# FF2 by seven block products in five chunks, with partial sums through DRAM

## The chip, the cores and the metric

The kernel runs on one core of a Trainium2 chip. The metric is the device time of one launch in microseconds, as a median of 3 runs. The kernel computes in fp32: TensorE multiplies numbers of a shorter format (fp32r), so each fp32 operand is split into a high and a low part, and each product takes three matmuls: high × high, high × low, low × high.

## The reference

One layer of a hybrid decoder on 512 tokens, width 2048. The change touches the channel sub-layer at its end:

```
h = rms_norm(x, g_pre_mlp) * (1 + sc2) + sh2
f = square(relu(h @ w_ff1)) @ w_ff2        # w_ff1: 2048 x 8192, w_ff2: 8192 x 2048
x = x + gt2 * rms_norm(f, g_post_mlp)
```

Below, FF1 is `h @ w_ff1`, `u` is its squared ReLU, FF2 is `u @ w_ff2`. Everything before (the attention and recurrence branches, their output projection) is the same in both kernels.

## The kernel before

**FF1** already uses a scheme of seven block products (after Strassen and Winograd): a 2×2 block matrix product takes 8 block products, or 7 if sums and differences of the blocks are formed first and the 7 results are added up afterwards. The two token halves (256 tokens each) and the two halves of the 2048 inputs make one operand; the weights of a *pair* of 128-wide column blocks make the other. There are 32 pairs. Products 1 and 2 need no token-side sums; for pairs 0 to 11 they are made early (kind "a", and a part before it), and the five others later (kind "b"). Pairs 12 to 31 make all seven at once (kind "c").

A *step* is one pair and a quarter of the inputs: `raw_load(s + 3)` asks for its weights three steps ahead, `forms(s + 2)` (L1273 to L1297) makes the weights' forms two steps ahead, and `group(s)` (L1328) issues the matmuls, 42 of 128x256 for kind "c", 30 for "b". The forms are: three sums on VectorE (L1290, L1293, L1294), the high parts on ScalarE (L1289, L1296), the low parts on VectorE (L1295, L1297). The high and low tiles `fh`, `fl` have two buffers each, so that ScalarE can write the forms of step s + 2 only when TensorE is done with step s. At a pair's end `pair_end` (L1347) adds up the products, applies ReLU and square, and writes `u` to DRAM (`ud`).

**FF2** is the plain product: for each of 2 halves of the output columns, 64 blocks of 128 rows of the weights, 2 blocks of 512 columns and 4 blocks of 128 tokens, three matmuls of 128x512 (`f2_mm`, L1439 to L1446), 3072 in all. The 8 PSUM banks hold the 8 sums of one half from its first block to its last. `u` is read back and split by `u_split` (L1436, L1437), the weights by L102 and L103. Beside FF2's first half VectorE also makes the dot products of `qdot` (L218) that give the modulation vectors. After the last matmul of each block of tokens `final` (L1464) scales the row and adds the residual, 16 instructions of 128x512.

The program is written in the order of the loops. A scheduler then chooses the order on each engine ahead of the run; on the chip each engine takes its own list in that order, and an instruction that waits holds up those behind it on the same engine. SyncE (SP) issues the loads, GpSimd (POOL) the writes of `u`.

Of the kernel before, what the change touches and what calls it, by code (L numbers as in the profile page):

```python
# [30 lines left out]
NA1, NA2, NMS, NFS, NTMP, NXI, NPC, NSB, TD, MRATE, NMD, NRT = 4, 8, 22, 18, 6, 4, 2, 11, 3, 0.8, 4, 6  # L31
NL = 2
# [98 lines left out]
def hybrid_block_kernel(ctx: ExitStack, tc: tile.TileContext, xT, c, vec, wada, wst, win, wv0, wv1,  # L131
# [1013 lines left out]
    def alpha_end(q, p, pool, tg, nb):  # L1145
        A.activation(P1[q], p[:, T1], AF.Copy)
        x = pool.tile([128, 256], F32, name="ax", tag=tg, bufs=nb)
        u = pool.tile([128, 256], F32, name="au", tag=tg, bufs=nb)
        V.tensor_add(x, p[:, T2], P1[q])
        relu2(q, 0, x, 1.0, u)  # L1150
        G.dma_start(ud[q][:, 0, T1], u)
# [161 lines left out]
    def open_banks(s):  # L1313
        if s >= len(GR) or GR[s] in asked:
# [251 lines left out]
```

## Time and profile before

| what | value |
|---|---|
| median of 3 runs | 2247.62 us (2246.13 to 2249.41) |
| profiled execution: its own time | 2245.18 us |
| profiled execution: span, first to last instruction | 2243.5 us |
| mean granted clock of TensorE | 0.986 of full speed |
| FF1's seven-product steps, last window | 1120 to 1518 us |
| FF2's matmuls | 1523.6 to 2234 us |
| end after the last matmul | 9.1 us |

The profile is of one execution. Times are microseconds unless marked ns. PE is TensorE's matmul side, PEld its weight loads, DVE is VectorE, ACT ScalarE. In a window's row, the first number after the stretch is its length, then each engine's busy time with its count of instructions; PEclk is the granted clock (1.00 is 2.4 GHz, 0.50 is 1.2 GHz). In a timeline's row the bracket gives the idle time ahead of the instruction and what ended it. Names like `fh` are buffers of the program, written output<-inputs; `ps_...` are PSUM banks.

### The profile page before, as it was taken

What the parts mean: (1) busy time and instruction counts of PE and PEld (TensorE: products, weight loads), DVE (VectorE), ACT (ScalarE), POOL (GpSimd) and SP (SyncE); (2) the same over time, 40 slices, a digit from 0 to 9 for tenths busy, and PEclk for the clock granted to TensorE, in tenths of its full rate; (3) what the DMA queues carried; (4) which work ended last, traced back from release to release, by engine and by line L of the source; (5) the groups of instructions that cost most, each with busy time, mean ns of one, the idle gap of its engine ahead of it and who ended that gap; (6) DMA issues with size and microseconds to landing.
All of it is one profiled execution on the core that took longest, in us unless ns stands there. A gap on an engine that the chain in (4) does not pass through costs nothing.

```text
span 2243.5 us, 33596 instructions
## 1 busy us (share of the span) xinstructions
PE 2161.5 (96%) x12317; PEld 1853.6 (83%) x12317; DVE 1590.0 (71%) x3260; ACT 1144.2 (51%) x2139; POOL 40.5 (2%) x81
## 2 busy tenths in 40 slices
PE   7997999999989988999999999998999999999998
PEld 3686878878867867999999999997888888888886
DVE  8977999878886768799988888876654334333333
ACT  4348889559983237655555555554323333333331
POOL 0000000000000000000000000000000000000000
PEclk9999999999999999999999999999999999999999
DMA  9755545741238885655544434437877444444433
GB/s 378 309 219 157 177 157 170 242 148 59 72 103 273 286 266 167 192 171 177 178 131 138 135 123 134 139 133 258 300 244 229 141 144 146 143 143 146 143 122 113
DMA packets 138982, 398.41 MB, mean 178 GB/s; under 512 B 18609, under 2 KB 19777, under 8 KB 134465
## 3 DMA queue, kind: packets, MB, share of 16 engines
q1 hardware_dynamic: 132546, 375.31, 51.5%
q0 software_dynamic: 6272, 20.98, 2.5%
q8 instruction: 96, 1.57, 0.3%
q14 instruction: 68, 0.56, 0.1%
HBM read 366.84 MB, written 29.38 MB: 177 GB/s over the span
## 4 chain that ended last, share of the span: by engine, by line
PE 66%; issue 24%; DVE 5%; ACT 3%; DMA 1%; POOL 0%; DVEq 0%; SPq 0%; POOLq 0%; ACTq 0%
PE ps_pj L1445 4%; PE ps_pj L1444 4%; PE ps_pj L1446 4%; PE ps_pj L1131 3%; PE ps_pj L1132 3%; PE ps_pj L1133 3%; PE ps_T L1446 3%; PE ps_T L1444 3%; PE ps_S L1445 3%; PE ps_S L1444 3%; PE ps_S L1446 3%; PE ps_T L1445 3%; PE ps_T L1131 2%; PE ps_T L1133 2%; PE ps_T L1132 2%
## 5 line engine op out<-in xcount | busy, mean ns | idle before, releaser
L102 ACT ACTIVATE sl<-wr 128x512 fp32r<-128x512 f32 (+2 forms) x388 | 228.9, 613 | 342.4 <-DMA wr<-wout 91.4
L103 DVE TENSOR_TENSOR sl<-wr,sl 128x512 fp32r<-128x512 f32 (+2 forms) x388 | 256.1, 671 | 188.2 <-ACT sl L102 173.8
L218 DVE SCALAR_TENSOR_TENSOR md<-md,ca 128x512 f32<-128x512 f32 x256 | 170.2, 686 | 59.2 <-DMA md<-wada 38.4
L1289 ACT ACTIVATE fh<-fr 128x768 fp32r<-128x768 f32 (+1 forms) x128 | 87.3, 682 | 227.7 <-PE ps_T L1132 89.6
L177 PE MATMUL ps_pj<-AH,sl 128*128 128x512 f32 x384 | 161.7, 421 | 0.0
L1297 DVE TENSOR_TENSOR fl<-fs,fh 128x1024 fp32r<-128x1024 f32 x128 | 156.4, 1222 | 3.7 <-ACT fh L1296 3.6
L103 DVE TENSOR_TENSOR AL<-wr,AH 128x512 fp32r<-128x512 f32 x120 | 81.7, 689 | 108.6 <-ACT AH L102 108.6
L102 ACT ACTIVATE AH<-wr 128x512 fp32r<-128x512 f32 x120 | 73.5, 626 | 164.2 <-PE ps_O L1446 68.4
L178 PE MATMUL ps_pj<-AL,sl 128*128 128x512 f32 x384 | 153.2, 399 | 0.0
L179 PE MATMUL ps_pj<-AH,sl 128*128 128x512 f32 x384 | 153.0, 398 | 0.0
L1437 DVE TENSOR_TENSOR AL<-ur,AH 128x1024 fp32r<-128x1024 f32 x64 | 78.4, 1224 | 103.9 <-ACT AH L1436 103.6
L1295 DVE TENSOR_TENSOR fl<-fr,fh 128x768 fp32r<-128x768 f32 (+1 forms) x128 | 96.5, 754 | 53.2 <-ACT fh L1289 53.1
L1296 ACT ACTIVATE fh<-fs 128x1024 fp32r<-128x1024 f32 x128 | 133.6, 1044 | 0.0
L1436 ACT ACTIVATE AH<-ur 128x1024 fp32r<-128x1024 f32 x64 | 67.7, 1058 | 83.7 <-PE ps_T L1445 79.6
L1132 PE MATMUL ps_pj<-tlt,fh 128*128 128x256 f32 x368 | 103.7, 282 | 0.0
L1131 PE MATMUL ps_pj<-AH,fh 128*128 128x256 f32 x352 | 99.1, 282 | 0.0
L1133 PE MATMUL ps_pj<-AH,fl 128*128 128x256 f32 x352 | 98.4, 280 | 0.0
L1290 DVE TENSOR_TENSOR fs<-fr 128x512 f32<-128x512 f32 x128 | 88.2, 689 | 5.2 <-DMA fr<-wff 2.1
L1444 PE MATMUL ps_pj<-sl,AH 128*128 128x512 f32 x204 | 81.4, 399 | 5.5 <-ACT sl L102 5.5
L179 PEld LDWEIGHTS ps_pj<-AH,sl 128*128 128x128 f32 x384 | 72.5, 189 | 16.3 <-DVE sl L103 0.6
L177 PEld LDWEIGHTS ps_pj<-AH,sl 128*128 128x128 f32 x384 | 72.8, 190 | 11.7 <-ACT tr L818 0.6
L1445 PE MATMUL ps_pj<-sl,AH 128*128 128x512 f32 x204 | 81.4, 399 | 0.5 <-DVE sl L103 0.5
(567 smaller groups left out, 6821.7 us busy)
## 6 DMA issues: line engine op xcount, KB each, us to landing
fr<-wff SPq DMA_DIRECT2D x144, 512.0 KB, 3.6
md<-wada SPq DMA_DIRECT2D x256, 256.0 KB, 4.9
wr<-wff SPq DMA_DIRECT2D x128, 512.0 KB, 3.8
ur<-ud SPq DMA_DIRECT2D x64, 512.0 KB, 3.4
wr<-win SPq DMA_DIRECT2D x48, 512.0 KB, 3.4
ada<-wada SPq DMA_DIRECT2D x22, 1024.0 KB, 10.3
wr<-wout SPq DMA_DIRECT2D x36, 512.0 KB, 4.7
ud<-ust POOLq DMA_DIRECT2D x20, 512.0 KB, 3.0
```

The source lines that it names most:

```text
L102: self.nc.scalar.activation(hi, raw, AF.Copy)
L103: self.nc.vector.tensor_sub(lo, raw, self.f(hi))
L177: T.matmul(o, wh, mh, start=start, stop=False)
L179: T.matmul(o, wl, mh, start=False, stop=stop)
L218: (V.scalar_tensor_tensor(w, w, 0.5, CA[0], op0=OP.mult, op1=OP.mult, accum_out=dq[s_][:, q_, k:k + 1]))
L1131: T.matmul(o, wh, b[0], start=start, stop=False, skip_group_check=True)
L1132: T.matmul(o, wh, b[1], start=False, stop=False, skip_group_check=True)
L1133: T.matmul(o, wl, b[0], start=False, stop=stop, skip_group_check=True)
L1297: V.tensor_sub(lo[:, 768:], Sm, f(hi[:, 768:]))
L1444: T.matmul(p, AH[:, k, hs], w[0], start=start, stop=False)
L1445: T.matmul(p, AH[:, k, hs], w[1], start=False, stop=False)
L1446: T.matmul(p, AL[:, k, hs], w[0], start=False, stop=stop)
```

## The change

FF2 also becomes seven block products. Its 32 pairs of rows of `u` are taken in five chunks (7, 7, 7, 7 and 4 pairs); in each chunk four groups of output columns n follow one another, so there are 20 groups, each of as many steps as the chunk has pairs: 128 steps (kind "f"). A step makes seven products of two token blocks with three matmuls of 128x256 each: 42, in all 5376. The seven sums of a group stand in 7 PSUM banks of the 8.

- **Between groups.** At a group's last step every sum is copied out of PSUM by ScalarE and written to DRAM by a DMA on POOL's queue (`bank_out`). The next group's banks are opened (`bank_open`): in the first chunk by a copy of 256 zeros, in the other four by a copy of the partial sum of the same n from the chunk before, which a DMA on ScalarE's queue has read back from DRAM (`p_in`, three buffers `pin`). The matmuls then add to what stands in the bank. In the last chunk `fin_step` adds the seven sums up instead of copying them out.
- **Weights.** `raw_load` and `forms` run over FF1's and FF2's steps in one list. For FF2 a step's high parts are one instruction of 128x1792 on ScalarE, and so are the low parts on VectorE.
- **Token side.** `pair_end` makes FF2's sums of `u` at the end of each of FF1's pairs (three new instructions on VectorE), and writes seven blocks, 917 KB a pair, to DRAM in place of four. `u_form` reads them back and splits them, one instruction of 128x1792 on ScalarE and one on VectorE for each pair: for pair 0 inside FF1, for six at FF2's start and in the first group, for the others in the last group of the chunk before.
- **End.** All 16 instructions of the final scaling stand after the last matmul.

```diff
--- before
+++ after
@@
-NA1, NA2, NMS, NFS, NTMP, NXI, NPC, NSB, TD, MRATE, NMD, NRT = 4, 8, 22, 18, 6, 4, 2, 11, 3, 0.8, 4, 6
-NL = 2
+NA1, NA2, NMS, NTMP, NXI, NPC, NSB, TD, MRATE, NMD, NRT = 4, 8, 22, 6, 4, 2, 11, 3, 0.8, 4, 6
+NPS, NFT, NXF = 5, 3, 6
...
-    ud = [dram.tile([128, 2, S], F32, name=f"ud{q}") for q in range(32)]
+    ud = [dram.tile([128, 1792], F32, name=f"ud{q}") for q in range(32)]
...
+    CH = [[*range(7 * i, 7 * i + 7)] for i in range(4)] + [[*range(28, 32)]]
+    for c_, pairs in enumerate(CH):
+        for n in range(4):
+            GR += [("f", (c_, n), p_) for p_ in pairs]
...
+        hi = wp.tile([128, 1792], F32R, name="fh", tag="fh", bufs=2)
+        lo = wp.tile([128, 1792], F32R, name="fl", tag="fl", bufs=2)
         FM[s] = hi, lo
+
+        def part(src, c0, n):
+            A.activation(hi[:, c0:c0 + n], src, AF.Copy)
+            V.tensor_sub(lo[:, c0:c0 + n], src, f(hi[:, c0:c0 + n]))
...
+        V.tensor_add(Sm[:, 1024:1536].rearrange("p (a b) -> p a b", a=2),
                      R[:, 256:768].rearrange("p (a b) -> p a b", a=2),
                      R[:, None, :256].to_broadcast([128, 2, 256]))
-        V.tensor_add(Sm[:, 512:768], Sm[:, :256], R[:, 512:768])
-        V.tensor_add(Sm[:, 768:], Sm[:, 512:768], R[:, 768:])
-        V.tensor_sub(lo[:, :n], R[:, 256:256 + n], f(hi[:, :n]))
-        A.activation(hi[:, 768:], Sm, AF.Copy)
-        V.tensor_sub(lo[:, 768:], Sm, f(hi[:, 768:]))
+        V.tensor_add(Sm[:, 1536:1792], Sm[:, 1024:1280], R[:, 512:768])
+        V.tensor_add(Sm[:, 1792:], Sm[:, 1536:1792], R[:, 768:1024])
+        if one and kind != "b":
+            part(R[:, 256:], 0, 1792)
+        else:
+            n = 256 if kind == "b" else 768
+            part(R[:, 256:256 + n], 0, n)
+            part(Sm[:, 1024:], 768, 1024)
...
+        V.tensor_sub(X[:, 4:6], X[:, 1:3], X[:, 0:1].to_broadcast([128, 2, 256]))
+        V.tensor_add(X[:, 6], X[:, 4], X[:, 2])
+        V.tensor_sub(X[:, 7], X[:, 6], X[:, 3])
...
+    FORD = (1, 2, 6, 7, 4, 5, 3)
...
+    def u_form(p_, sl):
+        u_load(p_)
+        u = UR.pop(p_)
+        hi, lo = US[p_] = SL[sl]
+        A.activation(hi, u, AF.Copy)
+        V.tensor_sub(lo, u, f(hi))
+        SLOT_OF[p_] = sl
...
+    def p_in(c_, n, i):
+        t_ = OPP["p"].tile([128, S], F32, name="pin", tag="pin", bufs=3)
+        nc.scalar.dma_start(t_, pd[n, i])
+        PI_[c_, n, i] = t_
+
+    def bank_open(c_, n, i):
+        b_ = PB2[c_, n, i] = bank()
+        if c_ == 0:
+            A.activation(b_[:, T2], zz, AF.Copy)
+        else:
+            A.activation(b_, PI_.pop((c_, n, i)), AF.Copy)
+
+    def bank_out(c_, n, i):
+        b_ = PB2.pop((c_, n, i))
+        t_ = OPP["p"].tile([128, S], F32, name="pst", tag="pst", bufs=NPS)
+        A.activation(t_, b_, AF.Copy)
+        G.dma_start(pd[n, i], t_)
...
+    def f2_mm(s, i):
+        _, (c_, n), p_ = GR[s]
+        l = FORD[i]
+        hi, lo = FM[s]
+        uh, ul = US[p_]
+        b_ = PB2[c_, n, i]
+        wc = slice(256 * SLOT[l], 256 * SLOT[l] + 256)
+        first, last = p_ == CH[c_][0], p_ == CH[c_][-1]
+        for t_ in range(2):
+            o = b_[:, 256 * t_:256 * t_ + 256]
+            c0 = 256 * UB[l] + 128 * t_
+            uh_, ul_ = uh[:, c0:c0 + 128], ul[:, c0:c0 + 128]
+            T.matmul(o, uh_, hi[:, wc], start=first and c_ == 0 and t_ == 0, stop=False, skip_group_check=True)
+            T.matmul(o, uh_, lo[:, wc], start=False, stop=False, skip_group_check=True)
+            T.matmul(o, ul_, hi[:, wc], start=False, stop=last, skip_group_check=True)
...
+            raw_load(s + 3)
+            forms(s + 2)
+            nq = (c_, n + 1) if n < 3 else (c_ + 1, 0)
+            if g == pairs[-2] and 0 < nq[0] < 5:
+                for i in range(3):
+                    p_in(*nq, i)
+            for i in range(7):
+                if g == pairs[0] and (c_, n, i) not in PB2:
+                    bank_open(c_, n, i)
+                f2_mm(s, i)
+                if g == pairs[-1]:
+                    if nq[0] < 5:
+                        bank_open(*nq, i)
+                        if nq[0] and i < 4:
+                            p_in(*nq, i + 3)
+                    if c_ < 4:
+                        bank_out(c_, n, i)
+                    else:
+                        fin_step(n, i)
...
+            if c_ == 0 and n == 0 and g < 5:
+                u_form(next(uord), frees.pop(0))
+                u_load(g + 3)
+            elif n == 2 and g == pairs[-1] and c_ < 4:
+                u_load(CH[c_ + 1][0])
+                u_load(CH[c_ + 1][1])
+            elif n == 3 and c_ < 4:
+                nx = CH[c_ + 1]
+                i = g - pairs[0] - (c_ == 3)
+                if 0 <= i < len(nx):
+                    u_form(nx[i], SLOT_OF[g])
+                    if i and i + 1 < len(nx):
+                        u_load(nx[i + 1])
+            if c_ < 3:
+                if qn < 64:
+                    qn += 1
+                    qdot(OPP["p"], 5, 1, ("pst", NPS))
...
-    def u_split(i):
-        if i < 64:
-            r_ = slice(2 * (i % 4), 2 * (i % 4) + 2)
-            u = UR.pop(i)
-            A.activation(AH[:, r_], u, AF.Copy)
-            V.tensor_sub(AL[:, r_], u, f(AH[:, r_]))
...
-    def f2_mm(h, m, fb, ch, free, start, stop):
-        w = ws.get(uf2[h, m], fb, free)
-        k = m % 8
-        hs = slice(128 * ch, 128 * ch + 128)
-        p = OB[fb, ch]
-        T.matmul(p, AH[:, k, hs], w[0], start=start, stop=False)
-        T.matmul(p, AH[:, k, hs], w[1], start=False, stop=False)
-        T.matmul(p, AL[:, k, hs], w[0], start=False, stop=stop)
...
+        rs = rs_of(FIN["p"], ssqf[:, ch])
+        for q in range(4):
+            mv = FIN["M"][:, ch, fbs(q)]
+            V.scalar_tensor_tensor(mv, mv, rs, XI.pop(0), op0=OP.mult, op1=OP.add)
+            nc.sync.dma_start(out[ch, :, fbs(q)], mv)
```

The first place is ScalarE in FF2. Before, its list holds the splits of `u` (`ur`) and of the weights (`wr`), nothing else:

```order
L1436 ACTIVATE AH_68<-ur_20279 128x1024
L102 ACTIVATE AH_68<-wr_20331 128x512 x2
L102 ACTIVATE AH_68<-wr_20365 128x512 x2
L1436 ACTIVATE AH_68<-ur_20347 128x1024
L102 ACTIVATE sl_20443<-wr_20395 128x512
L102 ACTIVATE sl_20459<-wr_20395 128x512
```

After, between two groups of the second chunk (line numbers are those of the changed kernel; `pst` takes a sum out, `pin` brings a seed in, `pd` is its place in DRAM, `fh_18664` is the high part of the weights two steps after the group's last):

```order
L1459 ACTIVATE pst_18681<-ps_S_18246 128x512
L1459 ACTIVATE pst_18694<-ps_T_18259 128x512
L1454 ACTIVATE ps_S_18690<-pin_18613 128x512
L1454 ACTIVATE ps_T_18703<-pin_18615 128x512
L1446 DMA pin_18692<-pd_9261 128x512
L1446 DMA pin_18705<-pd_9261 128x512
L1303 ACTIVATE fh_18664<-fs_18602 128x1792
L1459 ACTIVATE pst_18707<-ps_S_18272 128x512
L1459 ACTIVATE pst_18720<-ps_T_18285 128x512
L1454 ACTIVATE ps_S_18716<-pin_18679 128x512
L1454 ACTIVATE ps_T_18729<-pin_18692 128x512
L1446 DMA pin_18718<-pd_9261 128x512
```

Between the first two copies out and the others now stands the making of a weight form; two of the seven seeds' loads are issued ahead of it and one behind it, in ScalarE's list.

The second place is VectorE at the end of a pair of kind "b" in FF1. Before:

```order
L1362 TENSOR_TENSOR X_10988<-ps_O_10747,p1_5_9215 128x256
L1293 TENSOR_TENSOR fs_11033<-fs_11033,fr_10976 128x256
L1364 TENSOR_TENSOR X_10988<-ps_S_10748,X_10988 128x512
L1295 TENSOR_TENSOR fl_10979<-fr_10929,fh_10978 128x256
L1365 TENSOR_TENSOR X_10988<-ps_T_10749,X_10988 128x512
L1297 TENSOR_TENSOR fl_10979<-fs_10980,fh_10978 128x1024
L1366 TENSOR_TENSOR X_10988<-ps_S_10748,X_10988 128x256
```

After, at the same pair, from its last sum out of PSUM on (`uf` is the tile that `X` was, L1399 and L1400 are what L1365 and L1366 were):

```order
L1399 TENSOR_TENSOR uf_10824<-ps_T_10759,uf_10824 128x2x256
L1400 TENSOR_TENSOR uf_10824<-ps_S_10758,uf_10824 128x256
L1315 TENSOR_TENSOR fs_10984<-fs_10984 128x256
L1304 TENSOR_TENSOR fl_11042<-fs_10984,fh_11041 128x256
L1316 TENSOR_TENSOR fs_10984<-fs_10984 128x256
L1312 TENSOR_TENSOR fs_11039<-fs_11039 128x512
L1315 TENSOR_TENSOR fs_11039<-fs_11039 128x256
L1411 TENSOR_TENSOR uf_10824<-uf_10824 128x512
L1316 TENSOR_TENSOR fs_11039<-fs_11039 128x256
L1412 TENSOR_TENSOR uf_10824<-uf_10824 128x256
L1304 TENSOR_TENSOR fl_11042<-fs_10984,fh_11041 128x1024
L1413 TENSOR_TENSOR uf_10824<-uf_10824 128x256
```

L1411, L1412 and L1413 are new; the last two stand on either side of a low part of the weights (L1304) that TensorE's next steps read.

## Rows read from the trace of the kernel before

**Rows 1.** The top of the page: the span; busy time, share and instructions.

```profile
span 2243.5 us, 33596 instructions
...
PE 2161.5 (96%) x12317; PEld 1853.6 (83%) x12317; DVE 1590.0 (71%) x3260; ACT 1144.2 (51%) x2139; POOL 40.5 (2%) x81
```

**Rows 2.** Windows of FF1 and FF2, columns as in the first line.

```profile
core 0: us, PE busy (x) PEld busy (x) DVE busy (x) ACT busy (x) POOL busy (x), PEclk, DMA share, GB/s
950.00:1120.00 170.00, 169.92 (x1432) 169.92 (x1433) 163.04 (x288) 90.68 (x155) 12.32 (x23) 1.00 0.57 176
1120.00:1518.00 398.00, 398.00 (x3363) 397.93 (x3361) 330.75 (x473) 208.66 (x294) 11.18 (x21) 1.00 0.42 132
1518.00:1523.50 5.50, 0.14 (x2) 0.00 (x0) 2.38 (x5) 3.63 (x6) 0.53 (x1) 0.79 0.32 102
1523.50:1528.00 4.50, 3.86 (x8) 2.77 (x9) 4.32 (x6) 2.76 (x6) 0.00 (x0) 0.50 0.81 254
1528.00:2234.40 706.40, 706.22 (x3065) 574.51 (x3063) 301.57 (x479) 224.91 (x348) 0.00 (x0) 1.00 0.55 175
2234.40:2243.50 9.10, 0.00 (x0) 0.00 (x0) 3.65 (x7) 0.90 (x3) 0.00 (x0) 0.70 0.66 247
```

**Rows 3.** Windows, a stretch of FF2 with more transfers.

```profile
1555.00:1700.00 145.00, 145.00 (x631) 118.09 (x631) 86.32 (x184) 43.13 (x66) 0.00 (x0) 1.00 0.83 273
```

**Rows 4.** Timeline of PE at the start of FF2: start, us, instruction.

```profile
1523.59 0.80 PE L1444 MATMUL ps_pj<-sl,AH 128*128 128x512 f32 x1 [5.46 <-ACT sl L102]
...
1526.38 0.63 PE L1445 MATMUL ps_pj<-sl,AH 128*128 128x512 f32 x1
1526.81 0.63 PE L1446 MATMUL ps_pj<-sl,AL 128*128 128x512 f32 x1
```

**Rows 5.** Timeline of DVE, one step of FF1.

```profile
1492.49 0.43 DVE L1294 TENSOR_TENSOR fs<-fs,fr 128x256 f32<-128x256 f32 x1
```

**Rows 6.** Timeline of ACT, the same step and the next.

```profile
1493.19 0.85 ACT L1289 ACTIVATE fh<-fr 128x768 fp32r<-128x768 f32 x1 [3.18 <-PE ps_O L1132]
1493.94 1.04 ACT L1296 ACTIVATE fh<-fs 128x1024 fp32r<-128x1024 f32 x1
...
1498.16 0.85 ACT L1289 ACTIVATE fh<-fr 128x768 fp32r<-128x768 f32 x1 [2.91 <-PE ps_O L1132]
```

**Rows 7.** Groups of ACT by form: count | busy us, mean ns | idle before.

```profile
L1289 ACT ACTIVATE fh<-fr 128x768 fp32r<-128x768 f32 x80 | 67.3, 841 | 160.6 <-PE ps_O L1132 82.2 <-PE ps_T L1132 78.4
...
L1296 ACT ACTIVATE fh<-fs 128x1024 fp32r<-128x1024 f32 x128 | 133.6, 1044 | 0.0
...
L1324 ACT ACTIVATE ps_pj<-zz 128x256 f32<-128x256 f32 x31 | 11.6, 374 | 0.3
...
L847 ACT ACTIVATE y<-ps_pj 128x512 f32<-128x512 f32 x8 | 4.8, 594 | 0.0
```

**Rows 8.** Groups of DVE by form, the same columns.

```profile
L218 DVE SCALAR_TENSOR_TENSOR md<-md,ca 128x512 f32<-128x512 f32 x256 | 170.2, 686 | 59.2 <-DMA md<-wada 38.4 <-DMA ca<-cad 17.5 <-issue 2.5
L1297 DVE TENSOR_TENSOR fl<-fs,fh 128x1024 fp32r<-128x1024 f32 x128 | 156.4, 1222 | 3.7 <-ACT fh L1296 3.6
L1290 DVE TENSOR_TENSOR fs<-fr 128x512 f32<-128x512 f32 x128 | 88.2, 689 | 5.2 <-DMA fr<-wff 2.1
...
L1295 DVE TENSOR_TENSOR fl<-fr,fh 128x768 fp32r<-128x768 f32 x80 | 76.5, 956 | 53.0 <-ACT fh L1289 53.0
...
L1464 DVE SCALAR_TENSOR_TENSOR M<-M,rs,xin 128x512 f32<-128x512 f32 x16 | 11.0, 746 | 0.1
```

**Rows 9.** DMA issues: queue, count, KB each, median us to landing.

```profile
md<-wada SPq DMA_DIRECT2D x256, 256.0 KB, 4.9
...
ada<-wada SPq DMA_DIRECT2D x22, 1024.0 KB, 10.3
...
wr<-wff SPq DMA_DIRECT2D x16, 256.0 KB, 2.7
```

**Rows 10.** The 64 loads of md in FF2: time to landing.

```profile
DMA to landing us min/median/max: 3.8/5.6/7.2
```

More of the change, by code (lines that the diff above doesn't have):

```diff
@@ new lines, in hybrid_block_kernel, with u_load @@
+    SL = {i: (AHf[:, 1792 * i:1792 * i + 1792], ALf[:, 1792 * i:1792 * i + 1792]) for i in range(4)}
+    UR, US = {}, {}
+    ulist = [p_ for c_ in CH for p_ in c_]
+    def u_load(p_):
+        if p_ < 32 and p_ not in UR:
+            UR[p_] = uf_tile().rearrange("p a b -> p (a b)")[:, :1792]
+            nc.sync.dma_start(UR[p_], ud[p_])
+    def u_form(p_, sl):
[5 more added lines that the diff above has]
+        SLOT_OF[p_] = sl
@@ new lines, in hybrid_block_kernel, with tmp, v2, fin_step @@
+    FIN = {}
+    def tmp(name):
+        return FIN["p"].tile([128, S], F32, name=name, tag="tmp", bufs=NFT)
+    def v2(ap):
+        return ap.rearrange("p (a b) -> p a b", a=2)
+    def fin_step(n, i):
+        l = FORD[i]
+        b_ = PB2.pop((4, n, i))
+        M = FIN["M"]
+        d1, d2 = slice(256 * n, 256 * n + 256), slice(1024 + 256 * n, 1280 + 256 * n)
+        W_ = FIN["w"]
+        def done(j, half):
+            for t_ in range(2):
+                ch = 2 * j + t_
+                mv = M[:, ch, (d1, d2)[half]]
+                A.activation(tmp("sq")[:, :256], mv, AF.Square, accum_out=ssqf[:, ch, 2 * n + half:2 * n + half + 1])
+            mv = M[:, 2 * j:2 * j + 2, (d1, d2)[half]]
+            V.scalar_tensor_tensor(mv, mv, (1.0, -1.0)[half], gbc2[0][:, None, (d1, d2)[half]].to_broadcast([128, 2, 256]),
+                                   op0=OP.mult, op1=OP.mult)
+        if l == 1:
+            W_[1] = tmp("w1")
+            A.activation(W_[1], b_, AF.Copy)
+        elif l == 2:
+            V.tensor_add(M[:, 0:2, d1], v2(b_), v2(W_[1]))
+            done(0, 0)
+        elif l == 6:
+            V.tensor_sub(W_[1], W_[1], b_)
+        elif l == 7:
+            W_[3] = tmp("w3")
+            V.tensor_add(W_[3], b_, W_[1])
+        elif l == 4:
+            V.tensor_add(M[:, 0:2, d2], v2(b_), v2(W_[3]))
+            done(0, 1)
+        elif l == 5:
+            V.tensor_add(M[:, 2:4, d2], v2(b_), v2(W_[3]))
+            V.tensor_add(W_[1], b_, W_[1])
+            done(1, 1)
+        else:
+            V.tensor_add(M[:, 2:4, d1], v2(b_), v2(W_[1]))
+            done(1, 0)
@@ L1390, in hybrid_block_kernel @@
             hst.close()
-            FP2["p"] = gst.enter_context(tc.tile_pool(name="fp2", bufs=1, side="right", reuse_waits="tile"))
+            RP["p"] = pool(rst, "rp", side="right")
         open_banks(s + 2)
         forms(s + 2)
+        if RP and "u" not in RP and not any(v[1] is None for v in RAW.values()):
+            frs.close()
+            RP["u"] = pool(rst, "ufp", side="right")
         if kind == "a":
@@ L1491, in hybrid_block_kernel @@
-    u_split(63)
-    x1_load(0)
+            if kind == "b" and q == NA1 + NA2 - 1:
+                ast.close()
+                xst = ExitStack()
+                xp = pool(xst, "xp", side="right")
+                SL[4] = tuple(xp.tile([128, 1792], F32R, name=f"us4{x}") for x in "hl")
+            if q == 29:
+                u_form(0, 4)
+            if q == 30:
+                u_load(1)
     for ch in range(4):
```

225 lines of the change are left out of this document (112 added, 113 removed).

## The prediction

> **What bounds the kernel now.** I read the top of the page first: PE is busy 96% of a span of 2243.5 us, VectorE 71%, ScalarE 51% [rows 1]. So the span is the matmuls' time plus a few gaps, and the question for each stage is whether something else comes late there. The windows answer it [rows 2]. FF1's "c" steps (1120 to 1518) keep PE busy all of 398.00 us with 3363 matmuls of 128x256: 118.35 ns each. FF2 (1528 to 2234.4) keeps it busy 706.22 of 706.40 us with 3065 matmuls of 128x512: 230.5 ns each. PE's gaps around FF2 are 5.5 us ahead of it, some 4.5 us at granted clock 0.50 (1.2 GHz) right after, and 9.1 us behind it. The matmul rate decides both stages, and in both every form is ready in time.
>
> Who has room? In the "c" stretch ScalarE is busy 208.66 of 398 us (52%), VectorE 330.75 (83%); in the "b" stretch ahead of it (950 to 1120) VectorE has 163.04 of 170, 7 us free [rows 2]. In FF2 both have more than half free. Most of the arithmetic of the change is therefore paid for; what it changes is that FF2 gets seams.
>
> **FF2's matmuls.** Before: 3072 in 1523.5 to 2234.4, 710.9 us with the slow start. After: 5376 of 128x256, the shape and step (42 matmuls) of FF1's "c" pairs. 5376 × 118.35 ns = 636.2. Difference **−74.7**. A step takes 42 × 0.11835 = 4.97 us, which is also the distance of the two L1289 in [rows 6]; one product of a step takes 0.71.
>
> **FF2's start.** The 5.5 us ahead of FF2 are the first forms, made when FF1 has ended (PE waited 5.46 us for a split [rows 4]). Now they are made in FF1's last steps by the same list that feeds FF1: **−5** (0 to −5.5).
>
> **The seams, 16 with seeds.** Within a group a step is like a "c" step. At a group's end seven sums must leave their banks and seven seeds enter, on ScalarE, whose list is fixed. What a fixed list does is seen in one FF1 step: the sums were there at 1492.92 [rows 5], their split L1296 started at 1493.94, because L1289 ahead of it waited for PE to finish the step whose buffer it takes, to 1493.19 [rows 6]. The list of the changed kernel has at a seam: out 0, 1; open 1, 2; loads 4, 5; the form of step L + 2 (L is the group's last step); out 2, 3; open 3, 4; load 6; then out 4, 5, open 5, out 6, open 6. That form has the place of L1289: it waits until PE has ended step L, since `fh` has two buffers. So five copies out and four openings stand behind the moment E at which L ends, and PE goes on meanwhile into L + 1.
>
> Durations: the form of 128x1792 on ScalarE 1.044 + 3 × 0.203 = 1.65 (0.203 is the difference of the 1024 and 768 rows [rows 7]); a copy out 0.59 as the 128x512 row out of PSUM; a copy in 0.37 for 256 [rows 7], for 512 estimated 0.58. Then, after E: form to 1.7; out 2 to 2.3, out 3 to 2.9, open 3 to 3.45. L + 1 wants bank 3 at 3 × 0.71 = 2.13: 1.3 to 1.4 late. Open 4 to 4.05, in time for the shifted product. Out 4, 5, open 5 to 6.15, wanted at 4.9: 1.3 late. Load 6 is issued at about 4.4; loads of 256 KB landed in 2.7 us in one place [rows 9] and in 5.6 (at most 7.2) in FF2 [rows 10]: the seed is there at 7.1 to 10.0, bank 6 open at 7.7 to 10.6, wanted at 6.9: 0.8 to 3.7 late. Sum 3.5 to 6.4 a seam. I take 6.0, by the loads in FF2, since the stage is loaded at least as much now. 16 × 6.0 = **+96** (56 to 102; each engine in order, so nothing gives a gain). In the last chunk's three seams the final sums stand in place of the copies out; I count them alike.
>
> **Three seams with zeros** (first chunk): copies out as above, but no load; what is late is bank 3 and bank 5, with 0.37 in place of 0.58: some 2 each, **+6** (0 to 15).
>
> **Chunk turns.** 31 pairs of `u` get their forms within FF2, five or six in a row, one a step. VectorE per step: sums 0.69 + 0.43 + 0.43 [rows 5, 8], low part of 1792 = 1.222 + 3 × 0.266 = 2.02 (the rows for 1024 and 768 differ by 0.266 [rows 8]), in all 3.57; the low part of `u` adds 2.02, a `qdot` 0.69: 5.6 to 6.3 us where PE needs 4.97. That is 0.6 to 1.3 us lost a step once the two steps' lead is used up: 31 × 0.62 = 19, 31 × 1.3 = 40, less what the lead saves in five places. Transfers there: 7 × (0.52 + 0.92) MB of weights and `u` plus 3.7 MB of sums out and in = 13.8 MB in 35 us of matmuls. 273 GB/s went with a DMA share of 0.83 [rows 3], so all engines busy would be 329 GB/s: 42 us. The two overlap. **+18** (0 to 35).
>
> **The clock.** After 5.5 us with hardly a matmul the next window shows a granted clock of 0.50, and a matmul of 128x512 every 0.43 us (1526.38, 1526.81) where 0.23 is usual [rows 2, 4]: nine matmuls × 0.2 = 1.8 us lost. A seam's idle comes in three pieces of 1 to 4 us, so not each will drop the clock: 16 × 1.0 = **+16** (0 to 29).
>
> **FF1.** Each "b" pair gets three more VectorE instructions, 0.69 + 0.42 + 0.42 = 1.53 us (the 512 row, and the 256 form twice). 12 × 1.53 = 18.4, where 7 us are free: **+14** (11.4 to 18.4). VectorE has 17% free in the "c" stretch, but there the additions sit between low parts that PE waits for, 20 pair ends × 0.3 = **+6** (0 to 7). Both only cost: PE has no idle left to give back there.
>
> **The end.** 12 more of the final instructions behind the last matmul, 0.746 each [rows 8] = 9, and the last squares: **+10** on the 9.1 there are.
>
> **Sum** on the profiled execution: −74.7 − 5 + 96 + 6 + 18 + 16 + 14 + 6 + 10 = +86.3; span 2243.5 + 86.3 = 2329.8. That execution took 2245.18, 1.7 more than its span, and the median of the runs is 2247.62, 2.4 above it: **2334 us**.
>
> **Rivals.**
> *A: the seams are hidden.* FF2 is as bound by matmuls as FF1. For it: the same shapes ran 398 us without a gap at ScalarE 52% busy [rows 2]. Against it: a form behind a wait for PE stands in the middle of ScalarE's list at each seam. −74.7 − 5 + 14 + 10 = −55.7: 2243.5 − 55.7 + 4.1 = 2192. It decides if out 2 to 6 are done within a step, which needs the form behind them. This is the other side: faster.
> *B: the seams cost their cheap end* (loads land in 2.7, clock and turns hidden): −74.7 − 5 + 56 + 14 + 10 = +0.3, 2248.
> *C: transfers bound the seams.* Seeds land as the 1 MB loads did, 10.3 us [rows 9], since they queue behind weights and sums. Bank 6 opens at 4.4 + 10.3 + 0.6 = 15.3, 8.4 late; a seam is 11.1, 16 × 5.1 = 82 more: 2416. For it: DMA share 0.83 in a stretch of FF2 now [rows 3]; against it: 256 KB loads in that same stretch landed in 5.6 [rows 10].
> *D: the clock stays at 1.2 GHz for the step after each seam.* 19 × 4.97 = 94 in place of 16: 2412. For it: the drop at FF2's start came from a single gap; against it: it lasted some 4.5 us, under one step, and came after 5.5 us of idle in one piece [rows 2]. The Trainium skill, "TensorE: Matmul & The Clock Gate", section "A second HAM failure mode: psum-queue depth-cycling", tells of a kernel that cycles through PSUM banks and whose short idle times between groups of matmuls were enough to make the clock swing between its two levels; by that rule D happens at each seam, and no stretch of the trace before has such groups.
>
> **How the numbers follow.** Forecast 0.75, A 0.07, B 0.06, C 0.07, D 0.05. Ends of the forecast's own range: seams at 56 with the clock's 0 give 2278, turns at 35 with the clock's 29, seams at 102 and FF1's upper ends 2375. A is left out of the range and about half of C and D; B is taken in: 2247 to 2410. A measurement of this kernel tells 0.2% (4.5 us) from no change: faster 0.09 (A and a part of B), same 0.04 (B), slower 0.87.
>
> **What would show it.** In the profile after: about 118 ns a matmul within a group; PE idle at 19 places, each some 6 us in three pieces, released by ScalarE's openings and, for the last bank, by the load of the seed; the granted clock below 1.00 only there; no gap between FF1 and FF2; a longer stretch of VectorE-bound steps at "b" pairs and in each chunk's last group. If ScalarE's openings are done before PE wants their banks, I am wrong in the largest term, and A or B holds. If the seeds' DMAs release nearly all of the idle time, C is right; if PE has no long idle but the clock reads 0.50 within steps, D.

## The result, and the profile after

The changed kernel took 2375.91 us (median of 4 runs, 2370.18 to 2385.83), the kernel before 2247.75 (4 runs). The ratio is 1.0575, 95% interval 1.0533 to 1.0617: slower, and by 128 us where 86 were forecast.

The top of the page after, for [rows 1]:

```profile
span 2369.5 us, 38792 instructions
...
PE 2150.9 (91%) x14621; PEld 1952.7 (82%) x14621; DVE 1877.2 (79%) x3528; ACT 1315.9 (56%) x2199; POOL 94.1 (4%) x181
```

PE has 2304 more matmuls and is yet busy 10.6 us less, but 91% of the span in place of 96%. The stretches that answer [rows 2], in its columns (the b pairs, the c pairs, the passage from FF1 to FF2, FF2, the end):

```profile
973.00:1137.00 164.00, 152.67 (x1231) 147.45 (x1229) 147.44 (x276) 81.56 (x145) 5.32 (x10) 1.00 0.55 188
1180.00:1540.00 360.00, 359.59 (x3037) 359.39 (x3036) 310.91 (x416) 185.70 (x201) 9.57 (x18) 1.00 0.46 158
1544.00:1551.00 7.00, 7.00 (x61) 7.00 (x60) 6.86 (x9) 4.47 (x6) 0.00 (x0) 1.00 0.83 263
1551.00:2338.60 787.60, 680.02 (x5341) 663.12 (x5339) 554.77 (x705) 396.30 (x459) 60.57 (x113) 0.95 0.65 219
2339.00:2369.50 30.50, 0.00 (x0) 0.00 (x0) 15.47 (x30) 3.51 (x16) 0.00 (x0) 0.55 0.68 224
```

The c pairs are full as before. At the passage PE works without a gap. In FF2 PE is busy 680.0 of 787.6 us at a mean clock of 0.95. After the last matmul's end follow 30.8 us, where it was 9.3.

By stages of the profiled execution (126.0 us longer in span): up to the first b pair's end 5.5; b pairs 21.8 (from the first pair's end to the last's: 156.3 before, 178.2 after); c pairs 1.3; FF2 with its start 75.9 (716.1 from FF1's end to the last matmul's end, 792.0 after); the end 21.5. The first of these can't be put down to the change: the two programs have the same rows in the same order up to some 945 us, and in two kernels that are like the changed one so far (e10 and e2, below) it was 1.4 and 10.3.

FF2's 792.0 us are 636.2 for 5376 matmuls at full clock, 106.9 of idle PE (the 68 waits in the timeline added up), and a rest of 49. Of the rest, 11 belong to the waits too: the matmul ahead of a wait is shown for 0.28 us, where the next one would have started after 0.118. So waits cost 118 us. The other 38 are matmuls that follow one another more slowly than at full clock. The idle time, in the waits of PE (total, times, longest):

```profile
PE ps_T L1477 <- DVE fl L1304: 32.0, 9, 8.6
PE ps_pj L1477 <- DVE fl L1304: 20.0, 10, 4.9
PE ps_S L1477 <- DVE fl L1304: 13.2, 10, 3.4
PE ps_pj L1476 <- ACT ps_pj L1454: 11.8, 11, 2.9
PE ps_S L1476 <- ACT ps_S L1454: 6.0, 6, 2.1
```

L1477 are the matmuls that take the weights' low part, L1476 the first ones, which wait for an opened bank (L1454). The prediction's waits at openings are there, 21 us in all banks, but the waits for low parts come to 70. Some 12 more are waits for high parts.

A seeded seam as predicted, in the fourth chunk. ScalarE's timeline (L1303 form, L1459 out, L1454 open, L1446 the seed's load):

```profile
2158.17 1.70 ACT L1303 ACTIVATE fh<-fs 128x1792 fp32r<-128x1792 f32 x1 [1.31 <-PE ps_pj L1478]
2159.78 0.58 ACT L1459 ACTIVATE pst<-ps_T 128x512 f32<-128x512 f32 x1
2160.25 0.59 ACT L1459 ACTIVATE pst<-ps_S 128x512 f32<-128x512 f32 x1
2160.73 0.60 ACT L1454 ACTIVATE ps_T<-pin 128x512 f32<-128x512 f32 x1
2162.57 0.60 ACT L1454 ACTIVATE ps_S<-pin 128x512 f32<-128x512 f32 x1 [1.24 <-DMA pin<-pd]
2162.60 0.33 ACTq L1446 DMA_DIRECT2D pin<-pd  x1
...
2168.81 0.60 ACT L1454 ACTIVATE ps_pj<-pin 128x512 f32<-128x512 f32 x1 [3.62 <-DMA pin<-pd]
```

and PE's waits in the same place:

```profile
2161.39 0.39 PE L1476 MATMUL ps_T<-fh,us4h 128*128 128x256 f32 x1 [0.74 <-ACT ps_T L1454]
...
2163.23 0.39 PE L1476 MATMUL ps_S<-fh,us4h 128*128 128x256 f32 x1 [0.86 <-ACT ps_S L1454]
...
2169.46 0.39 PE L1476 MATMUL ps_pj<-fh,us4h 128*128 128x256 f32 x1 [2.90 <-ACT ps_pj L1454]
```

The form starts when PE is done with the group's last step; out 2, out 3, open 3 follow; then the openings wait for seeds; the last seed, asked for at 2162.60, is used at 2168.81. PE loses 0.74, 0.86 and 2.90, three pieces, 4.5 us; the prediction had 1.4, 1.3 and 0.8 to 3.7.

What it did not have is seen in the first chunk, between groups without seeds. SyncE's issues, VectorE's rows, and PE's:

```profile
1594.20 1.65 SPq L217 DMA_DIRECT2D md<-wada  x3
1595.94 0.83 SPq L1291 DMA_DIRECT2D fs<-wff  x1
1596.94 6.66 SPq L217 DMA_DIRECT2D md<-wada  x4
```

```profile
1599.38 0.69 DVE L218 SCALAR_TENSOR_TENSOR md<-md,ca 128x512 f32<-128x512 f32 x1 [3.06 <-DMA md<-wada]
...
1601.79 0.69 DVE L218 SCALAR_TENSOR_TENSOR md<-md,ca 128x512 f32<-128x512 f32 x1 [1.71 <-DMA md<-wada]
...
1602.99 0.69 DVE L218 SCALAR_TENSOR_TENSOR md<-md,ca 128x512 f32<-128x512 f32 x1 [0.50 <-DMA md<-wada]
...
1603.61 2.02 DVE L1304 TENSOR_TENSOR fl<-fs,fh 128x1792 fp32r<-128x1792 f32 x1
```

```profile
1605.69 0.58 PE L1477 MATMUL ps_T<-fl,AH 128*128 128x256 f32 x1 [4.94 <-DVE fl L1304]
```

The scheduler put seven `qdot` loads (L217) in a row at the seam. A load's tile belongs to the ring of the copies out (`pst`), so it waits for a copy's write to DRAM. The weights' load (L1291) stands between and behind them on SyncE, and on VectorE the low part (L1304) stands behind three dot products that wait for their data. PE idles 4.94 us. Over FF2 these two waits are, on SyncE and on VectorE:

```profile
SPq L217 <- DMA pd<-pst: 60.3, 34, 7.1
```

```profile
DVE fs L1312 <- DMA fs<-wff: 106.5, 54, 11.5
```

Not all of this waiting reaches PE. Traced back to VectorE's last idle time ahead of each late low part, 32 of the 70 us stand behind a dot product that waited for its data, 29 behind sums that waited for weights.

The clock: at such a wait the granted clock falls to 0.50 (1.2 GHz), and behind it the matmuls of 128x256 follow each other by 0.21 us, where 0.118 is usual. First the window around the wait of 4.94 us above, then PE's rows at another:

```profile
1604.80:1611.60 6.80, 5.91 (x27) 5.92 (x28) 6.80 (x13) 0.00 (x0) 0.00 (x0) 0.50 0.39 127
```

```profile
1962.84 0.58 PE L1477 MATMUL ps_T<-fl,AH 128*128 128x256 f32 x1 [5.39 <-DVE fl L1304]
...
1963.43 0.41 PE L1476 MATMUL ps_T<-fh,AH 128*128 128x256 f32 x1
1963.64 0.41 PE L1477 MATMUL ps_T<-fl,AH 128*128 128x256 f32 x1
```

The trace has 14 such stretches in FF2, 78 us in all.

PE's longest wait is no seam's. SyncE's issues, VectorE's row and PE's:

```profile
1963.23 0.39 SPq L1606 DMA_DIRECT2D ggd<-gg  x1
1965.04 20.70 SPq L1291 DMA_DIRECT2D fs<-wff  x3
```

```profile
1980.03 0.69 DVE L1312 TENSOR_TENSOR fs<-fs 128x512 f32<-128x512 f32 x1 [11.46 <-DMA fs<-wff]
```

```profile
1982.71 0.58 PE L1477 MATMUL ps_T<-fl,AH 128*128 128x256 f32 x1 [8.61 <-DVE fl L1304]
```

L1606 stores a modulation vector, 2048 single values, once in FF2. The weights' load issued 1.8 us behind it landed after 15.0 us, where 3.8 is the median. The kernel before has the same store; two loads issued in the two us behind it landed after 15.3 us, and PE did not wait. In e1, e5, e8, e9, e10 and e12 PE's longest wait stands beside this store too (6.0 to 11.3 us). No run moved the store, so that it is the cause is read from the order of events alone.

### The profile page after: what moved, and what is told of

Same layout as the page of the kernel before. It is cut to its first block, busy times and chain, and to the rows that moved or that the text cites. A ratio compares the mean times of both kernels' runs of the same rounds, so it can differ in the third digit from the quotient of the medians.

```text
span 2369.5 us, 38792 instructions
## 1 busy us (share of the span) xinstructions
PE 2150.9 (91%) x14621; PEld 1952.7 (82%) x14621; DVE 1877.2 (79%) x3528; ACT 1315.9 (56%) x2199; POOL 94.1 (4%) x181
## 4 chain that ended last, share of the span: by engine, by line
issue 37%; PE 29%; DVE 15%; DMA 12%; ACT 5%; POOL 1%; SPq 0%; DVEq 0%; POOLq 0%; ACTq 0%
DMA fs<-wff 7%; DVE fl L1304 5%; PE ps_pj L1132 2%; PE ps_pj L1133 2%; PE ps_pj L1134 2%; DVE fs L1312 2%; PE ps_T L1132 1%; PE ps_T L1134 1%; PE ps_T L1133 1%; DMA pin<-pd 1%; PE ps_S L1134 1%; PE ps_S L1133 1%; PE ps_S L1132 1%; ACT fh L1303 1%; POOL pd L1460 1%
## 5 line engine op out<-in xcount | busy, mean ns | idle before, releaser
L1303 ACT ACTIVATE fh<-fs 128x1792 fp32r<-128x1792 f32 (+2 forms) x302 | 420.6, 1400 | 512.7 <-PE ps_pj L1478 95.8
L1304 DVE TENSOR_TENSOR fl<-fs,fh 128x1792 fp32r<-128x1792 f32 (+2 forms) x302 | 496.5, 1649 | 122.9 <-ACT fh L1303 122.8
L1312 DVE TENSOR_TENSOR fs<-fs 128x512 f32<-128x512 f32 x254 | 174.0, 686 | 129.7 <-DMA fs<-wff 129.2
L103 DVE TENSOR_TENSOR sl<-wr,sl 128x512 fp32r<-128x512 f32 (+2 forms) x252 | 163.5, 662 | 48.4 <-ACT sl L102 33.7
L1477 PE MATMUL ps_pj<-fl,AH 128*128 128x256 f32 x432 | 126.1, 297 | 18.9 <-DVE fl L1304 18.7
L1478 PE MATMUL ps_pj<-fh,AL 128*128 128x256 f32 x432 | 124.7, 294 | 0.2 <-DVE AL L1437 0.2
L1476 PE MATMUL ps_pj<-fh,AH 128*128 128x256 f32 x432 | 118.5, 292 | 5.0 <-ACT fh L1303 2.4
L1315 DVE TENSOR_TENSOR fs<-fs 128x256 f32<-128x256 f32 x254 | 107.0, 422 | 5.6
L1316 DVE TENSOR_TENSOR fs<-fs 128x256 f32<-128x256 f32 x254 | 107.0, 422 | 5.1
L1477 PE MATMUL ps_T<-fl,AH 128*128 128x256 f32 x272 | 79.9, 294 | 29.5 <-DVE fl L1304 29.4
L1477 PEld LDWEIGHTS ps_pj<-fl,AH 128*128 128x128 f32 x432 | 87.6, 203 | 21.1 <-DVE fl L1304 21.1
L1477 PE MATMUL ps_S<-fl,AH 128*128 128x256 f32 x272 | 79.2, 291 | 12.4 <-DVE fl L1304 12.2
L1476 PEld LDWEIGHTS ps_pj<-fh,AH 128*128 128x128 f32 x432 | 83.5, 201 | 5.8 <-ACT fh L1303 2.8
```

Source lines behind the costliest of these rows:

```text
L103: self.nc.vector.tensor_sub(lo, raw, self.f(hi))
L1303: A.activation(hi[:, c0:c0 + n], src, AF.Copy)
L1304: V.tensor_sub(lo[:, c0:c0 + n], src, f(hi[:, c0:c0 + n]))
L1312: V.tensor_add(Sm[:, 1024:1536].rearrange("p (a b) -> p a b", a=2), R[:, 256:768].rearrange("p (a b) -> p a b", a=2), R[:, None, :256].to_ ...
L1476: T.matmul(o, uh_, hi[:, wc], start=first and c_ == 0 and t_ == 0, stop=False, skip_group_check=True)
L1477: T.matmul(o, uh_, lo[:, wc], start=False, stop=False, skip_group_check=True)
```

## The experiments

Each was timed beside the kernel before, in 4 runs (the no-seam one in 10). A ratio is to the kernel before; compare 1.0575 for the changed kernel. FF2 is its length in the profile, 792.0 in the changed kernel. In e3 and e4, whose FF2 differs from it at most in the residual's loads, it was 791.7 and 805.7, so some 14 us between two profiles can be chance.

**e1, the qdots' own tiles.**

```diff
-                    qdot(OPP["p"], 5, 1, ("pst", NPS))
+                    qdot(OPP["p"], 5, 1, ("md2", 2))
```

> The qdot tiles get two buffers of their own in place of the five that they share with the copies out of PSUM. Theory A (the weights come late: a qdot's load waits on SyncE for a copy's write to DRAM, and the weight loads stand behind it): the first three chunks lose no more than the fourth, some 22 us each in place of 41, so 45 to 60 us less: about 2320. Theory B (the prediction's: ScalarE's list, with a form behind PE's wait, makes the openings late): under 10 us less.

Measured: 2344.9 us, ratio 1.041 (1.0393 to 1.0426), FF2 760.5, 31 us less. PE's waits now:

```profile
PE ps_pj L1476 <- ACT ps_pj L1454: 17.2, 9, 4.5
PE ps_S L1476 <- ACT ps_S L1454: 14.6, 7, 8.3
PE ps_T L1477 <- DVE fl L1304: 13.4, 9, 3.4
```

Waits for low parts are halved (70 to 35 us in all banks), those for openings rise from 21 to 35; 8.3 of these stand beside the store L1606, which held up a low part before. The gain lies between the theories. Of theory A's cause only the shared ring holds: low parts behind a dot product that waits for its data fall from 32 us to 7, but VectorE's wait for weights does not fall (114 us, 106.5 before). So the dot products in VectorE's list were the larger cost of the ring, not the weights' loads behind SyncE's waits.

**e2, zeros for seeds.**

```diff
     def p_in(c_, n, i):
+        return
...
-            A.activation(b_, PI_.pop((c_, n, i)), AF.Copy)
+            A.activation(v2(b_), zz[:, None, :].to_broadcast([128, 2, 256]), AF.Copy)
```

> All banks are opened with zeros, no seed is read back, so the chunks' partial sums are not added up (left out). The copies out and their writes stay. Theory B: the seeds' share of a seam goes, 0.8 to 3.7 us at bank 6 and part of two openings, 16 times: 25 to 70 us less. Theory A: only the waits at openings go (21 us in the trace), 10 to 20 us less; the 5 us waits for low parts stay.

Measured: 2294.43 us, ratio 1.0184 (1.0161 to 1.0206), more than either theory had. FF2:

```profile
1551.80:2261.80 710.00, 661.33 (x5378) 649.68 (x5376) 555.29 (x710) 398.51 (x463) 60.84 (x113) 0.98 0.61 202
```

It is 82 us shorter. ScalarE makes as many copies into PSUM as before, 0.61 us each (0.60 before), so the price is not the copies but what is read back. PE's waits for openings fell from 21 to 4, for low parts from 70 to 34, and VectorE's wait for weights from 106.5 to 29.

**e3, token-side forms on GpSimd.**

```diff
-        V.tensor_sub(X[:, 4:6], ...
+        G.tensor_sub(X[:, 4:6], ...
```

and the two lines after it likewise.

> The three token-side instructions at each FF1 pair's end go from VectorE to GpSimd. Theory A (VectorE is full in the b pairs): the b stretch falls from about 179 us to 157 to 165, 14 to 22 us less in all. Theory B (GpSimd's own time or its access beside VectorE costs as much): no gain, or slower.

Measured: 2386.63 us, ratio 1.0595 (1.0574 to 1.0615): no gain; the b stretch grew from 178.2 to 191.3. GpSimd's row, then VectorE's sums of the weights in the b pairs, in this kernel and in the changed one:

```profile
L1411 POOL TENSOR_TENSOR uf<-uf 128x512 f32<-128x512 f32 x32 | 59.4, 1856 | 457.2 <-ACT uf L1407 286.7 <-ACT uf L1410 154.6 <-DVE md L218 15.9
```

```profile
L1312 DVE TENSOR_TENSOR fs<-fs 128x512 f32<-128x512 f32 x36 | 30.4, 844 | 18.6 <-DMA fs<-wff 18.3
```

```profile
L1312 DVE TENSOR_TENSOR fs<-fs 128x512 f32<-128x512 f32 x39 | 26.6, 685 | 15.0 <-DMA fs<-wff 15.0
```

The sums take 844 ns in place of 685 while GpSimd works beside them. The Trainium skill, "SBUF — State Buffer", section "Who interferes with whom", says that a VectorE instruction with two inputs in SBUF contends with a GpSimd instruction that reads SBUF; this trace agrees.

**e4, residual loads on ScalarE's queue**, 8 buffers in place of 6.

```diff
-            nc.sync.dma_start(t_, x1d[ch, :, fbs(q)])
+            nc.scalar.dma_start(t_, x1d[ch, :, fbs(q)])
```

> The residual's loads at the end go to ScalarE's queue, with 8 buffers, the first two blocks early, so that they do not stand behind the stores on SyncE. Theory A (the last 16 instructions wait for loads behind stores): the end after the last matmul falls from 31 to 20 to 23 us, 8 to 11 us less. Theory B (the instructions and stores themselves are the end): under 4 us less.

Measured: 2378.83 us, ratio 1.0553 (1.053 to 1.0577), inside the changed kernel's interval. The end fell from 30.8 to 26.6 us in the trace: nearer to theory B.

**e5, four tiles for weights and sums.**

```diff
-        R = RP["p"].tile([128, 2048], F32, name="fs", tag="fs", bufs=3)
+        R = RP["p"].tile([128, 2048], F32, name="fs", tag="fs", bufs=4)
```

> Four buffers in place of three for the tile that holds a step's weights and their sums; room for it is made by one buffer in place of two at the ends of the a pairs, zeros from a constant, and 4 in place of 6 residual buffers at the end. Theory C (the loop weights loaded, sums, high part, low part, next load has no slack: with three buffers a load is issued when the low part three steps before is done and must land within a step): FF1's b stretch falls from 178 to about 163 to 168 us, and FF2's 70 us of waits for low parts to under 35; 40 to 60 us less than the changed kernel, about 2325. Theory B (ScalarE's order at the seams): the b stretch as before, FF2 within 10 us.

Measured: 2362.73 us, ratio 1.0504 (1.0483 to 1.0526). The b stretch fell to 173.3 only, FF2 to 784.5, and the waits for low parts from 70 to 66. Theory C has some truth in the b pairs; in FF2 VectorE waited 108 us for weights, as before the edit (106.5), so a fourth tile did not bring the loads forward there.

**e6, seeds' loads on GpSimd's queue.**

```diff
-        nc.scalar.dma_start(t_, pd[n, i])
+        G.dma_start(t_, pd[n, i])
```

> The seeds' loads are issued on GpSimd's queue in place of ScalarE's. Theory D (zero seeds gave 80 us since a load that waits on ScalarE's list, for a buffer or for the sum's write, holds up the weights' high parts behind it): 25 to 60 us less. Theory E (the seeds cost by their landing time and by the transfers beside the weights' loads): within 10 us of the changed kernel, or slower, since the load now also stands behind the writes on GpSimd's list.

Measured: 2365.89 us, ratio 1.0518 (1.0493 to 1.0543), FF2 787.1: 10 us less, at the edge of theory E. The waits change places:

```profile
PE ps_T L1477 <- DVE fl L1304: 16.9, 11, 5.3
PE ps_S L1476 <- ACT ps_S L1454: 15.7, 5, 4.6
```

Low parts 39 us in all (70 before), openings 42 (21 before). That fits a load that waits on ScalarE's list and holds up forms behind it; once it is gone, PE waits for the seeds themselves.

**e7, add on the way out.** Banks opened with zeros; VectorE adds the earlier sum at the copy out.

```diff
+            t_ = PI_.pop((c_, n, i))
+            V.tensor_add(t_, b_, t_)
         G.dma_start(pd[n, i], t_)
```

> No seeds in PSUM: every bank is opened with zeros, and the earlier chunk's sum is added on the way out by VectorE (0.69 us each, 84 in the middle chunks, 28 in the last), from tiles loaded two steps before a group's end on GpSimd's queue; the qdot tiles have their own two buffers. The same result, with the seeds' latency off the start of a group. Theory E (landing time at a group's start): about 2290, near the zero seeds' 2294, since both 17 us of qdot gain and some 20 to 40 us of VectorE's additions come to it. Theory B': if VectorE's additions are late for the banks, 2330 to 2360.

Measured: 2326.59 us, ratio 1.0342 (1.0315 to 1.0368), FF2 747.9. The expectation of 2290 missed by 36 us; it is near the low end of B'. PE's waits for opened banks are nearly gone (3 us); those for low parts are 51. That VectorE's additions between them are the reason is likely, but no run took them out alone.

**e8, u's loads on GpSimd's queue.**

```diff
-            nc.sync.dma_start(UR[p_], ud[p_])
+            G.dma_start(UR[p_], ud[p_])
```

and the load in `pair_begin` likewise.

> All loads of u's forms (at the start of each b pair, and in FF2) are issued on GpSimd's queue in place of SyncE's; nothing else is changed. Theory F (head of the line on SyncE: such a load waits for its tile to be written out, and the weights' loads behind it come late): the b stretch falls from 178 us to 162 to 168, what VectorE's work alone makes of it (14.7 us busy a pair, 11 pairs), and FF2 gets 5 to 20 us shorter; 20 to 30 us less than the changed kernel. Theory G (VectorE's three added instructions are the cost of the b pairs): the b stretch stays at 174 or more.

Measured: 2368.45 us, ratio 1.0539 (1.0506 to 1.0571), not told apart from the changed kernel. The b stretch fell to 174.6, which is inside theory G's bound (174 or more) and 7 us above theory F's range; FF2 was 792.7, as before. Theory F alone fails.

**e9, accumulating writes**, with e1 and e8 in it.

```diff
+            G.dma_start(pd[n, i], t_, accum_op=OP.add)
```

> Banks of the first four chunks are opened with zeros and the copies out are added up in DRAM by accumulating DMAs on GpSimd's queue; only the last chunk is seeded from DRAM as before. The qdots have two tiles of their own, u's forms are loaded on GpSimd's queue. The same result as the reference. Theory E (the seeds' way back is the largest cost, 80 us, beside it the weights' loads behind waiting loads): the zero seeds' 2294 less 15 to 37 for the qdots and 10 to 15 for the b pairs, plus 4 seeded seams at 5: 2250 to 2285. Theory H (the seams cost by their copies and forms on ScalarE, and the zero seeds were fast since fewer bytes moved): an accumulation moves about what write and read did, so 2320 or more.

Measured: 2320.21 us, ratio 1.0307 (1.0288 to 1.0327), FF2 748.7: on H's side. The writes, what waits for them, and their landing:

```profile
L1461 POOL DMA_DIRECT2D pd<-pst x84: 849/1052/1476, 1746.9 to 2206.8; - x84
...
  DMA pd<-pst: 47.2, 15
...
DMA to landing us min/median/max: 3.5/8.2/19.3
```

An accumulating write lands in 8.2 us (4.5 for the plain one in the changed kernel), so ScalarE's copies out wait 47 us for a tile, and openings behind them make PE wait 33 us. Of these, one wait of 11.3 us, and the landing of 19.3, stand beside the store L1606.

**e10, nothing at the seams.** As e2, without the copies out, and with e1.

```diff
-                        bank_out(c_, n, i)
+                        PB2.pop((c_, n, i))
```

> Nothing leaves PSUM between groups and nothing is read back: every bank is opened with zeros (the sums of the first four chunks are left out of the result); qdots with two tiles of their own. What is left of FF2's loss is the turns, the qdots and the openings. Theory J (u's forms at the turns are hidden): FF2 640 to 665 us where the changed kernel has 792, in all 2225 to 2250. Theory K (VectorE and the transfers bound the turns, the prediction's 18 to 35): FF2 665 to 690, in all 2250 to 2275.

Measured: 2245.8 us, ratio 0.9976 (0.9964 to 0.9988). FF2:

```profile
1541.80:2213.70 671.90, 648.61 (x5378) 639.74 (x5376) 552.09 (x710) 345.51 (x351) 0.53 (x1) 0.99 0.53 170
```

671.9 lies in theory K's range for FF2; the whole time is 4 us under K's and inside J's. FF2 is 36 us above the matmuls (26 of waits, 10 of slow clock) for the turns, the qdots, the openings and the store L1606, beside which the longest wait, 6.0 us, stands. So with seams that cost nothing, the change just comes out even: 88.6 us, e1's 760.5 less 671.9, are the copies out and the seeds.

**e11, four tiles and u's loads on GpSimd's queue** (e5 with e8).

> Both earlier edits for the b pairs at once: four tiles for the weights and u's loads on GpSimd's queue. Theory I (the two hold each other's place: with three tiles a load must land within a step, with u's load ahead on SyncE it is late all the same): the b stretch 162 to 166 us, where each alone gave 173 to 175. Theory G (VectorE's added work and its order are the cost): 171 or more.

Measured: 2354.26 us, ratio 1.0459 (1.0421 to 1.0497). The b stretch is 168.6, between both theories. A stretch of the b pairs:

```profile
980.00:1130.00 150.00, 144.05 (x1181) 141.01 (x1180) 140.17 (x266) 76.83 (x137) 10.37 (x19) 1.00 0.60 198
```

VectorE is busy 93% (90% in the changed kernel); 9.0 of its idle 9.8 us still wait for weights.

**e12, forth and back.** Groups run through the columns in turns, so that four seams go.

```diff
+    def nn(c_, k):
+        return 3 - k if c_ % 2 else k
...
+                    if n == 3 and c_ < 4:
+                        PB2[nq[0], 0, i] = PB2.pop((c_, n, i))
```

> The groups run through the output columns forth and back, so that the last group of a chunk and the first of the next have the same columns: their sums stay in PSUM, and 4 of the 19 seams go, those at the turns. Beside it the accumulating writes, the qdots' own tiles, u's loads on GpSimd's queue and the residual's loads on ScalarE's. The same result as the reference. Theory L (a seam costs what zero seeds showed and a copy out that waits for a tile, 5 to 8 us, and the turns' seams most): 2280 to 2300. Theory M (the turns cost by u's forms, with or without a seam): 2305 or more.

Measured: 2299.65 us, ratio 1.0212 (1.0192 to 1.0232), at the edge of theory L's range. FF2:

```profile
1547.60:2270.70 723.10, 666.45 (x5378) 653.96 (x5376) 554.65 (x712) 360.10 (x407) 80.22 (x114) 0.97 0.68 199
```

25.6 us shorter than e9's. The whole time is 20.6 us shorter, 1.6 of it at the end, where the residual's loads moved. That makes 4.8 to 6.4 us for each of the four seams. It is the fastest of those that compute the whole, and slower than the kernel before.

## Why the prediction's time held, and which of its steps did not

- **Matmuls, −74.7, and the start, −5.** Right: at the passage PE is busy 7.00 of 7.00 us, and within a step matmuls follow by 0.118 us. These 80 us are what the change brings; e10 shows that the rest of the kernel eats them even without seams.
- **Seams, +96 and +6, and turns, +18: 120 us of idle PE.** Measured 118. That the sum fits is in part luck, for the time was lost in another place. The prediction walked along ScalarE's list alone and put 6.0 us on the openings of each of 16 seams; in the fourth chunk that walk is seen (form, outs, openings, last seed), at 4.5 us, but over all seams openings held PE up for 21 us. The 70 us at low parts came from lists that the walk lacked: VectorE's, where low parts stand behind dot products, and SyncE's, where loads into the copies' ring wait for writes to DRAM. The ring cost 31 us (e1), the seeds 82 (e2); the two prices overlap, so they are not added. By which way the seeds make the weights late, by ScalarE's list or by the transfers, stays open: e6 took their loads off that list and won 10 us. The traffic at the seams cost 88.6 us, clock included (e1 less e10); with the ring's 31 that is near the 118 which the prediction gave to the seams and the clock, but by another path. The turns' share was not measured alone; e10 bounds it, with qdots, openings and the store L1606, by 36.
- **The three seams with zeros, +2 each.** The step "no load; what is late is bank 3 and bank 5" failed. In each of the first chunk's three later groups PE waited 3.4 to 4.9 us for a low part, behind qdots.
- **The clock, +16.** Mis-sized: 38. The number of falls was about right, 14 where 16 were priced, though some came at waits within groups and one beside the store L1606. The price of a fall was wrong: 2.7 us each in place of 1.0, taken as a part of the 1.8 at FF2's start. The loss shrinks with the idle time (19 us in 7 stretches in e2, 10 in one in e10). Rival D had 94; two fifths of that came. The rule of the Trainium skill, "TensorE: Matmul & The Clock Gate", section "A second HAM failure mode: psum-queue depth-cycling", that short idle times swing the clock is borne out so far: it fell to 0.50 and rose again 14 times, and its mean over the stretch is 0.95.
- **b pairs, +14.** 22. VectorE's three instructions are counted rightly, but VectorE now also waits for weights (15.0 us in 157). Four tiles and u's loads off SyncE together give 9.6 us back; the 12.2 that stay lie within the forecast's 11.4 to 18.4. GpSimd is no way out (e3).
- **c pairs, +6.** 1.3: the additions are nearly hidden.
- **The end, +10.** 21.5. The step counted 12 instructions at 0.746. They also wait for the residual, 4.09 and 3.05 us at the worst:

```profile
2343.94 4.07 DVE L1645 SCALAR_TENSOR_TENSOR M<-M,rs,xin 128x512 f32<-128x512 f32 x6
...
2354.83 2.74 DVE L1645 SCALAR_TENSOR_TENSOR M<-M,rs,xin 128x512 f32<-128x512 f32 x4 [4.09 <-DMA xin<-x1d]
2360.61 0.75 DVE L1645 SCALAR_TENSOR_TENSOR M<-M,rs,xin 128x512 f32<-128x512 f32 x1 [3.05 <-DMA xin<-x1d]
```

  With six buffers the loads stand behind the stores on SyncE; e4, which moved them, gave back 4.2 of this in the trace, and nothing that the whole time shows. The final sums and squares of the last group, 5.4 us from the last matmul to the first of these instructions, were counted with 1 us beside what there was before.
- **Sum of the misses:** clock 22, idle −2, b 8, c −5, end 11.5, and 5.5 up to the first b pair's end, which may be chance: together 40, which is, but for rounding, the 39.7 between 126.0 and 86.3.
- **Rivals.** A fails (the seams aren't hidden). B's time came out only where the seams were taken away (e10). C fails as put: seeds landed in 4.7 us at the median, not 10.3, and moving their queue gave 10 us. The prediction's own sign, openings done before PE wants their banks, held for 90 of the 112 seeded openings. So its largest term was wrong as it was put, and yet neither A nor B came, since the waits for low parts took its place.

## What to carry to other kernels

Fewer multiplications pay only if the sums can stay where they are: here 20 groups of PSUM sums, with a way out and back at each change, cost more (88.6 us) than the saved matmuls (74.7). Where a seam adds transfers, walk every in-order list past it, SyncE's and VectorE's as well as that of the engine that makes the copies; a load into a ring that it shares with a slow write comes late, and so does all that stands behind its user. Price a fall of the clock by the whole slow stretch that follows, and look at the waits one by one: a sum of idle time can fit while its causes are others.

## What the runs showed of the hardware

- GpSimd's tensor operation of 128x512 took 1.86 us, and VectorE's sums beside it 0.844 in place of 0.685 (e3).
- An accumulating DMA of 256 KB took GpSimd 1.05 us to issue and landed in 8.2; the plain one 0.54 and 4.5 (e9).
- A stage that waits often runs slower also where it doesn't wait: in FF2 the granted clock was 0.50 in 14 stretches, 78 us in all, and matmuls that did not wait lost 38 us there.
- Loads issued in the two us behind a store of 2048 single values landed after 13 to 15 us (the kernel before, the changed one, e1, e5, e8, e10); a weights' load of the changed kernel lands after 3.8 at the median.
